# Banded attention's steps: projections ahead of scores, one product for the end, and a split moved from ScalarE to GpSimd

## The chip, the cores and the metric

The kernel runs on one core of a Trainium2 chip. The metric is the device time of one execution in microseconds (us); of several executions the median is told.

The engines have short names here: PE is TensorE, DVE VectorE, ACT ScalarE, POOL GpSimd and SP SyncE, which starts the DMAs. PEld is PE's loading of weights beside its matmuls.

## What is computed

The program holds two stacks of layers; the change touches one stage of the first, the odd layer with grouped-query attention in a window. Sizes: 1024 tokens, 256 context tokens, width 1024, 16 query heads on 4 key heads of dimension 64, query blocks of 128.

```python
def windowed_gqa(q, k, v, kc, vc, sink):
    ...
    s_ctx = jnp.einsum('bnqhgd,bchd->bnhgqc', qb, kc).astype(jnp.float32) * GQA_SCALE
    s_band = jnp.einsum('bnqhgd,bnkhd->bnhgqk', qb, kb).astype(jnp.float32) * GQA_SCALE
    ...
    valid = (jnp.abs(qpos - kpos) <= WINDOW) & (kpos >= 0) & (kpos < n)
    s_band = jnp.where(valid[None, :, None, None], s_band, -jnp.inf)
    s_sink = jnp.broadcast_to(sink[None, None, :, :, None, None], s_ctx.shape[:-1] + (1,))
    p = jax.nn.softmax(jnp.concatenate([s_ctx, s_band, s_sink], axis=-1), axis=-1).astype(v.dtype)
    ...
def odd_layer(h_lat, h_ctx, w_in, sink, w_out, rope, ctx_out):
    ...
    q, k, v, g = split_cols(h_lat @ w_in, ODD_SPLITS)
    q = apply_rope(q.reshape(b, n, GQA_KV_HEADS, GQA_GROUP, GQA_HEAD_DIM), *rope)
    ...
    y_l = (windowed_gqa(q, k, v, ck, cv, sink_hg) * jax.nn.silu(g)) @ w_out
```

## The kernel before

Numbers are float32, and each matrix product is made of three faster ones: a tensor x is split into a high half h (x rounded to a shorter type) and a low half l = x - h, and h*h, l*h and h*l are summed. So there are tiles in pairs: ah and al (features), whi and wlo (weights), kk and kl (keys), ph and pl (probabilities). `hi` (L162 on ACT, L164 on POOL) writes the high half and `lo` (L170) the low one.

The stage is `o1`, with `solo` set during attention. Keys, values and the first queries are projected ahead of it. Attention goes over 32 blocks (4 key heads by 8 query blocks); a block has 4 or 5 key tiles of 128 keys, and each key tile is one step of `attention`, 152 steps in all. A step puts together four kinds of PE work:

- D, scores: half-products of queries with keys (L1300 and L1301), eight for a block (four query heads of the group, with kk and with kl). They go into one of two PSUM buffers d. DVE adds the mask and takes the extreme (L1305); ACT takes the exponential (L1308, tile gw), and with that the buffer is free. `advance(want(n, i))` issues the halves, two or three in a step.
- F, projections: 28 products of queries or gates, each 24 matmuls of 512 columns (eight slices of the width by three halves; helper line L235), 4096 columns of fill for a product's accounts. `more` takes as many from the generator `fill` as a linear share of columns wants, three or six in a step (six where a step counts double). A product sums up in one PSUM bank f. A query is copied by ACT (L1113) and turned by POOL; a gate goes through tanh on ACT (L436) and a product on DVE (L437), and is written to DRAM (g_scr).
- V, values: two matmuls (L1328, L1329) with ph and pl into the bank o, of which there is one buffer.
- T, transposes: four (L1320) for the step two ahead, out of gw into the bank s; ACT makes ph (L162) and DVE pl (L170) from it.

After the exponentials of a step have been noted, `exps` issues them on ACT behind ph. When a block ends, `gqa_end` copies o into gatt (L1342, L1344) and adds up the sums of the exponentials in gden (L1348, L1349). Four blocks share one gden: it is transposed (L1354), turned into reciprocals (gdent), written to DRAM and read back spread over partitions, and POOL multiplies gatt by them (L1366).

`each`, called once in a step, is `add` in `o1`: it loads one gated feature (gate from g_scr, attention from am_scr), has POOL multiply the two (L1170), and in the next call `put` splits the product into ah and al for the output projection. The features of the first half of the tokens (c = 0) may start when `fill` puts them on the list `todo`, those of the second half (c = 1) when `fill` has come to its end. What is left after attention is done by a loop behind `self.solo = False`, then with products on DVE. The output projection's weights (`out_weights`: raw pieces by SP's DMAs, whi by ACT, wlo by POOL) follow, and its matmuls go into p.

PE, ACT and DVE carry out this stage in the order in which the code issues it (`in_order`); POOL's and SP's order is set by a scheduler.

Of the kernel before, what the change touches and what calls it, by code (L numbers as in the profile page):

```python
# [42 lines left out]
class Kern:  # L43
# [78 lines left out]
    def stg(self, n=512):  # L122
        return self.t(self.gp_, [P, 512], tag="stg", bufs=4)[:, 0:n]
# [175 lines left out]
    def attention(self, tiles, maxima, keys, prep, scores, values, end, want, fill, total, each, tail, late):  # L299


        steps = [(n, i) for n, t in enumerate(tiles) for i in range(len(t))]
        begin = [steps.index((n, 0)) for n in range(len(tiles))]
        G, U, done, cols, ahead, last, ends = {}, {}, 0, 0, [], None, iter(())

        def start(n):
            keys(n)
            G[n] = prep(n)

        def run(n):  # L310

            nonlocal done
            while n not in U:
                try:
                    next(G[n])
                    done += 1
                except StopIteration as e:
                    U[n] = e.value

        def advance(to):  # L320
            nonlocal done
            for n in range(len(tiles)):
                while done < min(to, sum(maxima[:n + 1])):
                    if n not in G:
                        start(n)
                    next(G[n])
                    done += 1

        def more(to):
            nonlocal cols  # L330
            while cols < to:
                n = next(fill, None)
                if n is None:
                    break
                cols += n
                if self.solo and cols % 4096 == 0 and to < total:
                    break
        for k in range(maxima[0] + maxima[1] - self.solo):
            if k == maxima[0] + min(self.R0, maxima[1]):
                run(0)  # L340
            advance(k + 1)
            more(cols + self.PRE * 512)
            self.exps()
        run(0)
        self.exps()
        first = cols

        share = [(2.0 if self.solo and i in (0, len(tiles[n]) - 2) else 1.0) for n, i in steps]
        whole = sum(share[:len(steps) - tail])
        for s in range(-2, len(steps)):  # L350
            swap = self.solo and s >= 0
            if self.solo and s >= 0:
                n, i = steps[s]
                advance(want(n, i))
                for m in range(n, len(tiles)):
                    if begin[m] - late <= s and m not in U:
                        run(m)
            if s + 2 < len(steps) and not swap:
                n, i = steps[s + 2]
                p, last = scores(U[n], tiles[n][i])  # L360
                ahead.append(p)
            if s < 0:
                continue
            n, i = steps[s]
            if not self.solo:
                advance(want(n, i))
            more(first + (total - first) * sum(share[:s + 1]) / whole)
            each()
            for m in range(n, len(tiles)):
                if begin[m] - late <= s and m not in U:  # L370
                    run(m)
            if i == 1 and not self.solo:
                with self.tc.issue_after(last):
                    next(ends, None)
            t = tiles[n]
            if i == 0:
                o = self.sps("o")
            values(o, U[n], t[i], i == 0, i == len(t) - 1, *ahead.pop(0))
            if i in (1, 2) and self.solo:
                next(ends, None)  # L380
            if i == len(t) - 1:
                ends = end(o, U[n])
                next(ends, None)
            if swap and s + 2 < len(steps):
                m, j = steps[s + 2]
                p, last = scores(U[m], tiles[m][j])
                ahead.append(p)
            self.exps()
        for _ in ends:
            pass  # L390
        more(total)
# [706 lines left out]
    def o1(self, act):  # L1098
# [9 lines left out]
        first = {}  # L1108
# [39 lines left out]
        mix = Act()  # L1148
# [3 lines left out]
        def add():  # L1152
            if made:
                k, c, gt = made.pop()
                self.put(mix, k, c, gt, "act", "pool" if k % 2 == 0 or self.solo else "dve")
                return
            kc = next((t for t in todo if t in self.ready), None)
            if kc is None:
                return
            todo.remove(kc)  # L1160
            k, c = kc
            ts = slice(*CH[c])
            gt = stg()
            self.dma(gt, g_scr[k * P:(k + 1) * P, ts])
            if k < 6:
                x = stg()
                self.dma(x, am_scr[k * P:(k + 1) * P, ts])
            else:
                x = self.last[c][:, k - 6]
            (nc.gpsimd if self.solo else V).tensor_tensor(gt, gt, x, ALU.mult)  # L1170
            made.append((k, c, gt))
# [42 lines left out]
        with self.in_order(), self.in_order(mybir.EngineType.Activation), self.in_order(mybir.EngineType.DVE):  # L1214
            self.gqa(gp, vv, k_scr, q_scr, am_scr, fill(), add)
# [5 lines left out]
        while todo or made:  # L1221
            add()
# [1024 lines left out]
```

## Time and profile before

| | us |
|---|---|
| median of 3 runs (2568.85 to 2571.87) | 2569.26 |
| profiled execution | 2569.92 |
| its span in the trace | 2568.1 |
| PE busy (share of the span) | 2391.3 (93%) |
| DVE busy | 1619.3 (63%) |
| ACT busy | 1112.8 (43%) |
| POOL busy | 938.6 (37%) |

The profile shows one execution. The busy times hold for the whole program, of which the attention stage lies from about 941 to 1398 us. A step of PE's work is followed on the time lines; what an engine waited for stands in square brackets behind the instruction that waited, with the time it was idle before it.

### The profile page before, as it was taken

The page shows a single profiled execution, that of the slowest core. Times are in us where ns is not written, and L with a number is a line of the kernel's source. Part 1 is how long each engine was busy: PE and PEld are TensorE (multiplying, and loading weights), DVE is VectorE, ACT ScalarE, POOL GpSimd, SP SyncE. Part 2 cuts the span into 40 slices and gives each one's busy share as a digit, 9 for nine tenths or more (in the row PEclk, how much of TensorE's full clock was granted, in tenths as well). Part 3 has the DMA queues.
Part 4 walks back from the last instruction along what each step waited for, and adds up shares of the span by engine and source line. Part 5 has one row for each costly group of instructions (what it writes and reads, how often), then busy time and mean ns, then how long its engine had stood idle before and what let it go on. Part 6 is the DMA issues. An engine that isn't in the chain of part 4 may idle for free. (4 is left out here: it accounts for less than half of the span.)

```text
span 2568.1 us, 36467 instructions
## 1 busy us (share of the span) xinstructions
PE 2391.3 (93%) x13014; PEld 1968.8 (77%) x13014; DVE 1619.3 (63%) x2732; ACT 1112.8 (43%) x2241; POOL 938.6 (37%) x776
## 2 busy tenths in 40 slices
PE   5999999999999998888887999999999999999998
PEld 3887777777678877776675879787777777799888
DVE  6785437788855546666665553558888577673455
ACT  4412226666653325555554323245666233513331
POOL 4304243354411145536333314046442343453231
PEclk9999999999999999999999999999999999999999
DMA  7465431132324221223214413233333232201433
GB/s 241 146 216 198 154 105 56 49 102 73 98 82 147 90 78 54 75 71 95 77 56 127 160 65 101 86 106 102 91 99 126 94 115 83 70 17 54 166 105 103
DMA packets 216693, 265.35 MB, mean 103 GB/s; under 512 B 42496, under 2 KB 142240, under 8 KB 216384
## 3 DMA queue, kind: packets, MB, share of 16 engines
q1 hardware_dynamic: 215792, 262.92, 32.5%
q8 instruction: 103, 1.69, 0.3%
q14 instruction: 78, 0.64, 0.1%
q10 hardware_dynamic: 720, 0.10, 0.0%
HBM read 188.83 MB, written 71.97 MB: 102 GB/s over the span
## 5 line engine op out<-in xcount | busy, mean ns | idle before, releaser
L170 POOL TENSOR_TENSOR wlo<-wraw,whi 128x512 fp32r<-128x512 f32 (+3 forms) x229 | 311.6, 1370 | 661.8 <-ACT whi L162 588.3
L162 ACT ACTIVATE whi<-wraw 128x512 fp32r<-128x512 f32 (+3 forms) x261 | 155.0, 613 | 346.7 <-DMA wraw<-in_even_w_in 50.8
L235 PE MATMUL f<-ah,whi 128*128 128x512 f32 x416 | 170.7, 410 | 7.5 <-DVE mixg L437 5.9
L170 DVE TENSOR_TENSOR pl<-pf,ph 128x512 fp32r<-128x512 f32 (+1 forms) x176 | 143.7, 817 | 41.3 <-ACT pf L1009 40.5
L235 PE MATMUL f<-ah,wlo 128*128 128x512 f32 x416 | 166.9, 401 | 0.0
L235 PE MATMUL f<-al,whi 128*128 128x512 f32 x416 | 166.4, 400 | 0.0
L162 ACT ACTIVATE ph<-s 128x512 fp32r<-128x512 f32 x152 | 90.8, 598 | 158.2 <-PE s L1320 157.2
L170 DVE TENSOR_TENSOR pl<-s,ph 128x512 fp32r<-128x512 f32 x152 | 104.4, 687 | 85.0 <-ACT ph L162 82.8
L1009 ACT ACTIVATE ph<-s 128x512 fp32r<-128x512 f32 (+1 forms) x176 | 101.5, 577 | 104.3 <-PE s L1006 103.3
L971 DVE TENSOR_REDUCE mx<-p 128x1 f32<-128x512 f32 (+1 forms) x208 | 116.8, 575 | 33.8 <-PE p L970 32.5
L235 PE MATMUL s<-ah,whi 128*128 128x512 f32 (+1 forms) x328 | 130.6, 398 | 3.9 <-ACT ah L545 3.2
L1305 DVE CUSTOM_DVE_ANT_0 d<-d,c_gqa_mask,nsink 128x640 f32<-128x640 f32 (+1 forms) x128 | 107.0, 853 | 39.1 <-PE d L1301 35.7
L235 PE MATMUL s<-al,whi 128*128 128x512 f32 (+1 forms) x328 | 128.8, 393 | 1.4 <-DVE al L547 1.4
L235 PE MATMUL s<-ah,wlo 128*128 128x512 f32 (+1 forms) x328 | 129.2, 394 | 0.0
L1696 DVE TENSOR_TENSOR_SCAN scu<-scu,ones_col 128x128 f32<-128x128 f32 (+3 forms) x64 | 97.6, 1538 | 14.1 <-ACT scu L1692 11.2
L1308 ACT ACTIVATE gw<-d,gm 128x640 f32<-128x640 f32 (+1 forms) x128 | 97.4, 765 | 14.1 <-DVE gm L1305 14.1
L1009 ACT ACTIVATE pf<-s 128x512 f32<-128x512 f32 (+1 forms) x176 | 100.9, 573 | 2.5 <-DVE pl L170 2.3
L1300 PE MATMUL d<-kk,qq 128*128 128x384 f32 (+1 forms) x128 | 48.5, 379 | 53.5 <-ACT gw L1308 46.1
L235 PEld LDWEIGHTS f<-ah,whi 128*128 128x128 f32 x416 | 79.3, 191 | 20.7 <-DVE mixg L437 8.5
L529 DVE CUSTOM_DVE_ANT_0 wmj<-wmt,srow,c_b_mod 128x1024 bf16<-128x1024 f32 x56 | 76.1, 1359 | 28.4 <-DMA wmt<-in_w_modT 26.1
L235 PEld LDWEIGHTS f<-ah,wlo 128*128 128x128 f32 x416 | 79.0, 190 | 17.7
L1320 PEld LDWEIGHTS s<-c_ident,gw 128*128 128x128 f32 x608 | 75.8, 141 | 21.1 <-DVE pl L170 0.5
(767 smaller groups left out, 7638.1 us busy)
## 6 DMA issues: line engine op xcount, KB each, us to landing
wmt<-in_w_modT SPq DMA_DIRECT2D x32, 512.0 KB
wraw<-in_even_w_in SPq DMA_DIRECT2D x56, 256.0 KB
wraw<-in_odd_w_in SPq DMA_DIRECT2D x48, 256.0 KB
wraw<-in_o_w_in SPq DMA_DIRECT2D x40, 256.0 KB
xold<-x_scr SPq DMA_DIRECT2D x40, 256.0 KB
mraw<-in_w_mod SPq DMA_DIRECT2D x16, 512.0 KB
x_scr<-x SPq DMA_DIRECT2D x32, 256.0 KB
mixx<-m_scr SPq DMA_DIRECT2D x30, 256.0 KB
```

What stands on the lines that cost most here:

```text
L162: nc.scalar.activation(out=out, in_=in_, func=AF.Copy)
L170: return e.tensor_tensor(out, in_, hi.bitcast(F32), ALU.subtract)
L235: self.nc.tensor.matmul(out, ws[:, k, c:c + m], a[k][ch], start=first and i == j == 0, stop=last and i == len(ks) - 1 and j == 2)
L529: V.tensor_tensor_reduce(out=junk, in0=w, in1=s[:, i], scale=0.5, scalar=self.bm[l][:, m, i:i + 1], op0=ALU.mult, op1=ALU.add, accum_out=s ...
L971: V.reduce_max(mx[:, e, j:j + 1], d[:, 0:y - x], axis=AX)
L1009: nc.scalar.activation(out=t, in_=s, func=AF.Exp, scale=MLA_SCALE)
L1300: mm(d[:, kw:kw + k1 - k0], qs, k[:, k0:k1], start=e == 0, stop=e == 1)
L1305: V.tensor_tensor_reduce(out=x, in0=x, in1=mask, scale=1.0, scalar=self.nsk[:, 4 * kv + g:4 * kv + g + 1], op0=ALU.add, op1=ALU.min, accum ...
L1308: self.pending.append(lambda w=w, x=x, g=g: nc.scalar.activation(out=w[:, 0:n], in_=x, func=AF.Exp, scale=-1.0, bias=m[:, g:g + 1], accum_ ...
L1320: self.nc.tensor.transpose(s[:, g * P:(g + 1) * P], W[g][:, x:x + P], self.ident)
L1696: V.tensor_tensor_scan(out=rev, data0=rev, data1=self.ones.to_broadcast([P, n]), initial=1.0, op0=ALU.mult, op1=ALU.mult)
```

## The change

In a step of the stage the projections (`more`) and the call of `each` now come ahead of the scores (`advance`); the loop that finishes a block's scores early, where they are due, stays behind them as before. In `attention` 4096 columns of `fill`, one product, are held back from the steps: the share that `more` asks for is capped, and behind the last step the end of the last block goes one part further (`next(ends)`), then `more(total + 1)` issues the kept product, and only then follows the transpose of the sums. As `fill` comes to its end only there, the features of the second half go on the list behind attention: all eight of them are made by the loop after it, where two were made inside before. Finally the high half of the features of the first half of the tokens is written by POOL in place of ACT: ACT has 8 instructions less, POOL 8 more; the two products that move out of the stage are on DVE now, not on POOL.

```diff
--- before.py
+++ after.py
@@ -347,14 +347,10 @@
 
         share = [(2.0 if self.solo and i in (0, len(tiles[n]) - 2) else 1.0) for n, i in steps]
         whole = sum(share[:len(steps) - tail])
+
+        held = 4096 if self.solo else 0
         for s in range(-2, len(steps)):
             swap = self.solo and s >= 0
-            if self.solo and s >= 0:
-                n, i = steps[s]
-                advance(want(n, i))
-                for m in range(n, len(tiles)):
-                    if begin[m] - late <= s and m not in U:
-                        run(m)
             if s + 2 < len(steps) and not swap:
                 n, i = steps[s + 2]
                 p, last = scores(U[n], tiles[n][i])
@@ -364,8 +360,10 @@
             n, i = steps[s]
             if not self.solo:
                 advance(want(n, i))
-            more(first + (total - first) * sum(share[:s + 1]) / whole)
+            more(first + (total - held - first) * min(1.0 if swap else 2.0, sum(share[:s + 1]) / whole))
             each()
+            if swap:
+                advance(want(n, i))
             for m in range(n, len(tiles)):
                 if begin[m] - late <= s and m not in U:
                     run(m)
@@ -386,6 +384,9 @@
                 p, last = scores(U[m], tiles[m][j])
                 ahead.append(p)
             self.exps()
+        if self.solo:
+            next(ends, None)
+            more(total + 1)
         for _ in ends:
             pass
         more(total)
@@ -1152,7 +1153,7 @@
         def add():
             if made:
                 k, c, gt = made.pop()
-                self.put(mix, k, c, gt, "act", "pool" if k % 2 == 0 or self.solo else "dve")
+                self.put(mix, k, c, gt, "pool" if self.solo else "act", "pool" if k % 2 == 0 or self.solo else "dve")
                 return
             kc = next((t for t in todo if t in self.ready), None)
             if kc is None:
```

PE, the step after one with three halves of scores. Before, the step's row begins behind four transposes (s): scores (d), six projections (f), values (o).

```order
L1320 MATMUL s_11754<-c_ident,gw_11616 128x128
L1300 MATMUL d_11765<-kk_10924,qq_11617 128x384
L1301 MATMUL d_11765<-kk_10924,qq_11617 128x256
L1300 MATMUL d_11765<-kl_10925,qq_11617 128x384
L1301 MATMUL d_11765<-kl_10925,qq_11617 128x256
L235 MATMUL f_11683<-ah_8655,whi_10606 128x512
L235 MATMUL f_11683<-al_8656,whi_10606 128x512
L235 MATMUL f_11683<-ah_8655,wlo_10607 128x512
L235 MATMUL f_11683<-ah_8661,whi_10606 128x512
L235 MATMUL f_11683<-al_8662,whi_10606 128x512
L235 MATMUL f_11683<-ah_8661,wlo_10607 128x512
L1328 MATMUL o_11716<-ph_11724,ovv_8682 128x512
```

After, in the like step (line numbers here are one higher than before), the projections stand directly behind the transposes.

```order
L1321 MATMUL s_11742<-c_ident,gw_11607 128x128
L235 MATMUL f_11715<-ah_8631,whi_10618 128x512
L235 MATMUL f_11715<-al_8632,whi_10618 128x512
L235 MATMUL f_11715<-ah_8631,wlo_10619 128x512
L235 MATMUL f_11715<-ah_8637,whi_10618 128x512
L235 MATMUL f_11715<-al_8638,whi_10618 128x512
L235 MATMUL f_11715<-ah_8637,wlo_10619 128x512
L1301 MATMUL d_11759<-kk_10918,qq_11608 128x384
L1302 MATMUL d_11759<-kk_10918,qq_11608 128x256
L1301 MATMUL d_11759<-kl_10919,qq_11608 128x384
L1302 MATMUL d_11759<-kl_10919,qq_11608 128x256
L1329 MATMUL o_11703<-ph_11711,ovv_8682 128x512
```

So six f rows have moved ahead of the d rows, and the values follow the scores.

PE, the end of the stage. Before, the values of the last two key tiles, then the transpose of the sums (gden) and the output projection (p):

```order
L1328 MATMUL o_13779<-ph_13787,ovv_8682 128x512
L1329 MATMUL o_13779<-pl_13788,ovv_8682 128x512
L1328 MATMUL o_13779<-ph_13805,ovv_8682 128x512
L1329 MATMUL o_13779<-pl_13806,ovv_8682 128x512
L1354 MATMUL s_13829<-c_ident,gden_13523 16x128
L235 MATMUL p_14005<-ah_13199,whi_13849 128x512
L235 MATMUL p_14005<-al_13200,whi_13849 128x512
```

After, the end of the kept product (its last 6 of 24 rows) stands ahead of the transpose of the sums:

```order
L235 MATMUL f_13786<-ah_8661,whi_12642 128x512
L235 MATMUL f_13786<-al_8662,whi_12642 128x512
L235 MATMUL f_13786<-ah_8661,wlo_12643 128x512
L235 MATMUL f_13786<-ah_8667,whi_12642 128x512
L235 MATMUL f_13786<-al_8668,whi_12642 128x512
L235 MATMUL f_13786<-ah_8667,wlo_12643 128x512
L1355 MATMUL s_13815<-c_ident,gden_13472 16x128
L235 MATMUL p_14005<-ah_13299,whi_13835 128x512
```

The transpose of the sums no longer follows the values but the 24 projections.

SP's queue, behind the reciprocals' DMAs (rec_scr) of the last key head's first half. wraw are raw pieces of the output weights, stg loads of features. Before:

```order
L129 DMA rec_scr<-gdent_13452 16x128
L129 DMA stg_13456<-rec_scr 64x4x128 x2
L129 DMA stg_13460<-rec_scr 64x4x128 x2
L129 DMA stg_13492<-g_scr 128x512
L129 DMA g_scr<-mixg_13488 128x512
L129 DMA stg_13494<-am_scr 128x512
L129 DMA stg_13551<-g_scr 128x512
L129 DMA wraw_13859<-in_o_w_out 128x2x256
L129 DMA stg_13603<-g_scr 128x512
L129 DMA wraw_13863<-in_o_w_out 128x2x256
```

After, from the second of the loads of reciprocals on:

```order
L129 DMA stg_13409<-rec_scr 64x4x128 x2
L129 DMA g_scr<-mixg_13430 128x512
L129 DMA stg_13461<-g_scr 128x512
L129 DMA stg_13463<-am_scr 128x512
L129 DMA stg_13520<-g_scr 128x512
L129 DMA stg_13522<-am_scr 128x512
L129 DMA stg_13577<-g_scr 128x512
L129 DMA stg_13579<-am_scr 128x512
L129 DMA stg_13638<-g_scr 128x512
L129 DMA stg_13684<-g_scr 128x512
L129 DMA wraw_13845<-in_o_w_out 128x2x256
L129 DMA wraw_13849<-in_o_w_out 128x2x256
```

The two pieces of weights, which stood between loads of features, now stand behind eight of them in a row.

ACT, at the same place. Before:

```order
L162 ACTIVATE ph_13504<-s_13499 128x512
L1308 ACTIVATE gw_13481,gs_13433<-d_13475,gm_13432 128x640
L162 ACTIVATE ah_13516<-stg_13492 128x512
L1342 ACTIVATE gatt_13522<-o_13388 64x2x128 x2
L162 ACTIVATE ph_13534<-s_13529 128x512
L162 ACTIVATE whi_13849<-wraw_13859 128x512
L162 ACTIVATE whi_13849<-wraw_13863 128x512
L162 ACTIVATE ph_13562<-s_13557 128x512
```

After:

```order
L437 ACTIVATE mixg_13604<-f_13457 128x512
L1343 ACTIVATE gatt_13471<-o_13504 64x2x128 x2
L162 ACTIVATE ph_13627<-s_13622 128x512
L162 ACTIVATE whi_13835<-wraw_13845 128x512
L162 ACTIVATE whi_13835<-wraw_13849 128x512
L162 ACTIVATE ph_13656<-s_13651 128x512
```

The feature's split (ah) is no longer between the exponential and the copy out of o (gatt); the splits of the weights (whi) stand as before between two splits of probabilities (ph).

## Rows read from the trace of the kernel before

**Rows 1.** Table by stretches: stretch, length, busy PE, PEld, DVE, ACT, POOL, clock, DMA.

```profile
941.00:1398.30 457.30, 388.18 (x2105) 319.72 (x2105) 281.26 (x573) 252.86 (x575) 196.75 (x188) 0.98 0.24 73
1363.60:1366.70 3.10, 3.08 (x9) 2.57 (x10) 3.07 (x6) 1.70 (x4) 2.17 (x2) 0.50 0.30 106
1397.40:1400.90 3.50, 3.00 (x7) 2.26 (x8) 1.99 (x4) 1.26 (x2) 0.00 (x0) 0.50 0.30 84
```

**Rows 2.** Waits from 935 to 1400 us: who waited for whom, total, times, longest.

```profile
PE d L1300 <- ACT gw L1308: 46.1, 30, 3.3
PE o L1328 <- DVE gatt L1344: 6.8, 5, 4.7
PE f L235 <- DVE mixg L437: 5.9, 11, 1.2
...
ACT ph L162 <- PE s L1320: 157.2, 109, 4.0
DVE pl L170 <- ACT ph L162: 82.8, 79, 3.3
```

**Rows 3.** Time lines of one step: start, length, engine, instruction, idle time before it.

```profile
1211.69 0.60 PE L1320 MATMUL s<-c_ident,gw 128*128 128x128 f32 x4
...
1212.82 0.79 ACT L1308 ACTIVATE gw<-d,gm 128x640 f32<-128x640 f32 x1
...
1213.75 0.44 PE L1300 MATMUL d<-kk,qq 128*128 128x384 f32 x1 [1.46 <-ACT gw L1308]
...
1214.44 0.39 PE L235 MATMUL f<-ah,whi 128*128 128x512 f32 x1
...
1215.83 0.40 PE L1328 MATMUL o<-ph,ovv 128*128 128x512 f32 x1
```

**Rows 4.** Time lines, the first of three borders between key heads.

```profile
1058.58 0.41 PE L1300 MATMUL d<-kk,qq 128*128 128x384 f32 x1 [1.16 <-POOL stg L450]
```

**Rows 5.** Groups of instructions: the gate's tanh and product (busy us, mean ns).

```profile
L436 ACT ACTIVATE mixg<-f 128x512 f32<-128x512 f32 x16 | 9.6, 597 | 7.7 <-PE f L235 7.6
L437 DVE SCALAR_TENSOR_TENSOR mixg<-mixg,f 128x512 f32<-128x512 f32 x16 | 11.0, 685 | 4.1 <-ACT mixg L436 4.0
```

**Rows 6.** Time lines: a feature's split on ACT, and values after it.

```profile
1361.11 0.63 ACT L162 ACTIVATE ah<-stg 128x512 fp32r<-128x512 f32 x1 [5.77 <-POOL stg L1170]
...
1363.62 0.77 PE L1328 MATMUL o<-ph,ovv 128*128 128x512 f32 x1 [4.71 <-DVE gatt L1344]
```

**Rows 7.** Time lines at the end of the stage.

```profile
1388.11 1.14 ACT L162 ACTIVATE whi<-wraw 128x512 fp32r<-128x512 f32 x2
...
1392.09 0.51 PE L1329 MATMUL o<-pl,ovv 128*128 128x512 f32 x1 [0.18 <-DVE pl L170]
...
1397.44 0.37 PE L1354 MATMUL s<-c_ident,gden 128*16 128x128 f32 x1 [4.85 <-DVE gden L1349]
...
1397.85 0.28 DVE L1356 TENSOR_SCALAR gdent<-s 16x128 f32<-16x128 f32 x1 [0.56 <-PE s L1354]
...
1398.27 0.77 PE L235 MATMUL p<-ah,whi 128*128 128x512 f32 x1 [0.46 <-ACT whi L162]
```

**Rows 8.** Time lines in the output projection: features' products, fourth weights, output 7.

```profile
1409.87 0.69 DVE L1170 TENSOR_TENSOR stg<-stg,stg 128x512 f32<-128x512 f32 x1
...
1421.54 1.15 DVE L1170 TENSOR_TENSOR stg<-stg,gatt 128x512 f32<-128x512 f32 x1 [0.84 <-DMA stg<-g_scr]
...
1434.02 2.67 POOL L170 TENSOR_TENSOR wlo<-wraw,whi 128x512 fp32r<-128x512 f32 x2 [7.51 <-ACT whi L162]
...
1435.95 0.39 PE L235 MATMUL p<-ah,whi 128*128 128x512 f32 x1
```

**Rows 9.** The small sums by line (ns min/median/max); scores behind the longest one.

```profile
L1349 DVE TENSOR_TENSOR gden<-gs,gm x30: 151/166/3036, 976.4 to 1381.3; 128x4 f32<-128x4 f32 x30
...
1159.99 0.39 PE L1300 MATMUL d<-kk,qq 128*128 128x256 f32 x1 [3.31 <-ACT gw L1308]
```

**Rows 10.** One line's answer: splits on POOL (ns min/median/max, first and last start).

```profile
L164 POOL TENSOR_SCALAR kk<-raw x9: 405/617/620, 973.8 to 1206.7; 128x512 fp32r<-128x512 f32 x6, 128x256 fp32r<-128x256 f32 x3
```

## The prediction

> **What bounds the kernel now.** Only the banded attention of the odd layer changes, so I read the stretch from its first step to the output projection. The table by stretches comes first: PE is busy 388.18 of 457.30 us at a granted clock of 0.98, ACT 252.86, DVE 281.26 [rows 1]. PE sets this stage and the other engines have room, so only PE's waits are to be won: 457.30 - 388.18 = 69 us, part of it small gaps. The list of waits names them. The largest by far is the first score matmul waiting for an exponential on ACT, 46.1 us in 30 waits; then value matmuls waiting for the o bank, 6.8 in 5, and projections waiting for the f bank, 5.9 in 11 [rows 2]. ACT for its part is idle 157.2 us for transposes and DVE 82.8 us for ACT [rows 2]: both wait for PE oftener than PE for them.
>
> The time lines show how one of the 30 waits comes about. Transposes start at 1211.69; the exponential that frees the score buffer runs from 1212.82 for 0.79 us; PE has finished its transposes and stands 1.46 us until the score matmul starts at 1213.75; the six projection matmuls behind it, which need nothing from ACT, start at 1214.44 and the values at 1215.83 [rows 3]. A block has two buffers for eight half-products, and the wait falls where a step with three halves is followed by the next step: once in a block.
>
> **Edit 1: projections ahead of scores.** What it moves: in each step F, D, V, T in place of D, F, V, T (projection, scores, values, transposes); on DVE the gate's product ahead of the score's reduction. Nothing is added. At the 30 places PE now does projections while the exponential ends. By the new order 24 of them have six projection matmuls ahead and 6 have three. Six take 1215.83 - 1214.44 = 1.39 us, three 0.70 [rows 3]. The wait is 1.46 [rows 3], so nearly all of it is covered: 24 x 1.39 + 6 x 0.70 = 37.6. At three borders between key heads a wait of 1.16 us of the same shape is put down to another releaser [rows 4]; each has three projections in the new order: 3 x 0.70 = 2.1. Together **-39.7 us**. The exponential itself stays where it is against the transposes: it follows them on ACT, and the reduction it waits for is DVE work on scores issued a step earlier. If it did come later by as much, nothing were won (second rival); above, the whole of the waits could go, 46.1 + 3.5 = 49.6.
>
> What the swap costs is at the borders of projection products. There is one f bank. The next product may start when ACT's tanh (0.597) and DVE's product (0.685) [rows 5] have read it; with hand-overs some 1.8 us after the last matmul has begun. Before, the scores and values stood in this gap; now a good part of that work stands ahead of the product's end, and the next product comes after two values (0.46) and transposes (0.60 [rows 3]), with D where there is one: 1.06 us and more. The 16 gate products at up to the longest wait seen, 1.2 [rows 2], give 19.2 at most against 5.9 now, that is +13.3; at best all 5.9 go. I take **+4**: most borders still have a part of V, T and D between them. The other bank, o, had 6.8 us of waits, of which 4.71 are one stall (edit 3) [rows 2, 6]; denser steps leave ACT and DVE less time to empty it: **+2**, with 0 and +6 as ends.
>
> **Edit 2: one product kept for the end.** 24 projection matmuls leave the loop, 24 x 0.232 = 5.6 us less there, and fill the stretch behind the last values. Before: last values at 1392.09, transpose of the sums after a wait of 4.85 at 1397.44, output projection at 1398.27 [rows 7], so 6.2 us. After: 0.2 + 23 x 0.232 = 5.6 to the last of the 24, 0.4 for its end, then what stands in a row: two splits of output weights on ACT, 1.14 [rows 7], which wait for the very weights that the kept product reads and stand ahead of its tanh, the tanh 0.60, the gate's product 0.69 [rows 5], the copy of the sums that DVE does behind it 0.28 and 0.2 of hand-overs: 8.9. The end gains 2.7 and the loop loses 5.6: -2.8. Besides, the clock: after the 4.85 us standstill the next 3.50 us ran at 0.50 [rows 1], that is 1.2 GHz; without standstill some 1.3 us of that come back. Together **-4.1**; between -6.6 (the splits find another place) and -1.5 (the clock falls all the same).
>
> **Edit 3: the high half of the first eight gated features on GpSimd.** Before, ACT stood 5.77 us ahead of such a split for GpSimd's product, and behind it in ACT's fixed order were the copies out of the o bank: PE's values waited 4.71 [rows 6], and 3.10 us then ran at 0.50 [rows 1], half of which is loss: 4.71 + 1.55 = 6.3 us that go. But the new wait stands near: GpSimd now has both halves, so the features come out more slowly, two more of them fall behind the reciprocals' DMAs, and on SP's queue the third and fourth piece of the first output weights now stand behind the features' loads. ACT's split of these pieces stands in its fixed order ahead of the next split of probabilities, so PE would wait again. No row shows it; it is bounded by 0 and by the stall that goes, 6.3; I take 2.5, nearer the lower end, since the pieces are asked for some microseconds ahead. Net **-3.8**.
>
> Later: the second eight features all fall behind the end in place of six. DVE's products there came at 1409.87 to 1421.54, five spacings, 2.33 us each [rows 8], so two more are 4.7. Behind them on GpSimd's list is the low half of the fourth output weights, which ran from 1434.02 for 2.67 us, to 1436.69, and its matmuls at output 7 started at 1435.95 without a wait, with no more than some 0.6 us of slack by what they read first [rows 8]. **+4.6**, between 0 (GpSimd takes the weights first) and 6.
>
> **Port of GpSimd and DVE.** The tiny sums on DVE take 0.166 us by median, but 3.04 us at the longest, where a GpSimd instruction runs beside it [rows 9]. PE's next score matmul then waited 3.31 in place of 1.46 [rows 9]: 1.85 paid. Eight more splits on GpSimd, 0.62 us each by the like split of keys [rows 10], add chances for this: **+1**, with 0 and 8 x 0.62 = 5 as ends. By the Trainium skill (SBUF — State Buffer, "SBUF: two separate sides") the port pair that GpSimd and DVE share is an exclusive lock: an instruction with two SBUF inputs on DVE stands until GpSimd's whole instruction is through, or the other way round. The trace agrees with its 3.04 us; by the rule's worst case the sum would be 4 us higher.
>
> **Sum.** -39.7 - 3.8 - 4.1 + 4 + 2 + 4.6 + 1 = -36.0. The profiled execution took 2569.92 (span 2568.1), the median of the three runs is 0.66 less: 2569.92 - 36.0 - 0.66 = **2533 us**.
>
> **Rivals.** *Nothing comes back:* the new waits at f, o and the fourth weights stay hidden, since ACT and DVE have idle time. The gain is 39.7 + 6.3 + 4.1 = 50.1 against the median: 2519. For it: ACT's 157.2 us of idle time [rows 2]; against: a single f bank, and half a microsecond of slack at the fourth weights. Chance 0.18.
>
> *The wait only moves:* the chain from exponential to reduction to the next exponential sets the step, and PE waits at F's end or at the values for what it waited for at the scores. Then only the end's 4.1 us remain: 2565, no difference that counts. Against it: DVE idles 82.8 us for ACT and ACT 157.2 for PE [rows 2], so neither is the bound of a block. Chance 0.07.
>
> *Slower, by the lock:* with the gate's product ahead of the reduction, DVE's sums at the block's end move against GpSimd's long products. If each of the 30 met one like the longest, PE would pay 30 x 1.85 = 55.5, less some 2.6 paid now: +53, so 2569.26 - 36 + 53 = 2586. From 36 / 30 = 1.2 us for a block on, the gain is gone. Against it: GpSimd is busy 196.75 of 457.30 us [rows 1], and the median sum is untouched. Chance 0.05.
>
> **How the numbers follow.** Forecast 0.70, the rivals 0.18, 0.07 and 0.05. The forecast's own ends: f between -5.9 and +13.3 and the other unknowns at their bounds, not all at once, 2522 to 2550. The range takes in the first rival with half of today's f waits gone, 2516, and on the other side 3 us more for an end of the f and o terms together: **2516 to 2553**. Within 0.2% is 5.1 us, about what can be told from no change. Faster 0.70 + 0.18 = 0.88, same 0.07, slower 0.05.
>
> **What would show it.** Score matmuls waiting for the exponential fall from 46.1 to about 10 us or less; the 4.71 stall at the values and ACT's 5.77 ahead of the feature split are gone; the stretch of 457.30 is near 417 to 420; 24 projections stand between the last values and the transpose of the sums, with the clock above 0.50 there; a wait of some 5 us appears at the fourth weights of output 7; projections' waits for the gate grow to about 10. I would be wrong if the exponentials start later against the transposes, if f waits pass 15 us, or if the tiny sums take over a microsecond on average.

## The result, and the profile after

The changed kernel took 2525.4 us, median of 6 runs (2520.4 to 2531.92), beside 2570.57 us for the kernel before: a ratio of 0.9824, with a 95% interval of 0.9808 to 0.984. That is 45 us or 1.8% faster. The forecast was 2533, with a range of 2516 to 2553.

The stage itself, from the first scores to the output projection (table by stretches: stretch, its length, busy time of PE, PEld, DVE, ACT and POOL, PE's clock, DMA):

```profile
944.65:1353.69 409.04, 384.45 (x2104) 315.35 (x2105) 281.58 (x572) 245.98 (x562) 196.25 (x191) 0.99 0.24 77
1354.60:1357.50 2.90, 2.90 (x8) 2.28 (x7) 0.00 (x0) 0.63 (x1) 0.95 (x1) 0.50 0.76 237
1397.71:1402.83 5.12, 5.12 (x14) 4.03 (x14) 3.98 (x6) 2.42 (x4) 2.56 (x2) 0.57 0.67 218
```

It takes 409.04 us in place of 457.30 [rows 1], with the same number of matmuls. The other two stretches are those with a lowered clock behind the start of the output projection and behind its wait at output 7. PE's waits from 935 to 1400 us (who waited for whom, total, times, longest):

```profile
PE f L235 <- DVE mixg L438: 8.5, 11, 3.4
PE p L235 <- ACT whi L162: 5.4, 1, 5.4
PE d L1301 <- issue: 5.2, 3, 3.7
PE d L1301 <- ACT gw L1309: 4.5, 6, 0.8
PE o L1329 <- DVE gatt L1345: 3.0, 5, 0.8
PE p L235 <- DVE gdent L1357: 2.4, 1, 2.4
...
PE o L1330 <- DVE pl L170: 2.0, 3, 1.6
```

Against [rows 2]: the scores' waits for the exponential are 4.5 us in 6 in place of 46.1 in 30, the o bank's 3.0 in place of 6.8, the f bank's 8.5 in place of 5.9. The 4.85 us at the transpose of the sums [rows 7] are gone. New are 2.4 us ahead of the output projection and 5.4 us at its output 7.

The place that answers to [rows 3], on the time lines (start, length, instruction):

```profile
1181.00 0.60 PE L1321 MATMUL s<-c_ident,gw 128*128 128x128 f32 x4
...
1181.35 0.48 PE L235 MATMUL f<-ah,whi 128*128 128x512 f32 x1
...
1182.13 0.79 ACT L1309 ACTIVATE gw<-d,gm 128x640 f32<-128x640 f32 x1
...
1183.06 0.44 PE L1301 MATMUL d<-kk,qq 128*128 128x384 f32 x1
...
1183.76 0.40 PE L1329 MATMUL o<-ph,ovv 128*128 128x512 f32 x1
```

The exponential starts 1.13 us after the transposes, as before (1212.82 - 1211.69), and the scores start 2.06 us after them, as before (1213.75 - 1211.69). In between six projections now run; the values follow the transposes by 2.76 us in place of 4.14.

The end of the stage, which answers to [rows 7]:

```profile
1345.10 0.50 PE L1330 MATMUL o<-pl,ovv 128*128 128x512 f32 x1 [0.17 <-DVE pl L170]
...
1351.04 0.27 PE L1355 MATMUL s<-c_ident,gden 128*16 128x128 f32 x1
1353.69 0.47 PE L235 MATMUL p<-ah,whi 128*128 128x512 f32 x1 [2.38 <-DVE gdent L1357]
```

From the last values to the output projection it is 8.59 us in place of 6.18. ACT and DVE in these 2.38 us do what was forecast, one behind the other:

```profile
1351.00 1.15 ACT L162 ACTIVATE whi<-wraw 128x512 fp32r<-128x512 f32 x2 [3.27 <-PE f L235]
1352.06 0.58 ACT L437 ACTIVATE mixg<-f 128x512 f32<-128x512 f32 x1
...
1352.67 0.69 DVE L438 SCALAR_TENSOR_TENSOR mixg<-mixg,f 128x512 f32<-128x512 f32 x1 [4.74 <-ACT mixg L437]
1353.28 0.27 DVE L1357 TENSOR_SCALAR gdent<-s 16x128 f32<-16x128 f32 x1
```

The fourth output weights and output 7, which answer to [rows 8]. The order of the lines is that of time; SPq is SP's DMA queue:

```profile
1386.16 0.95 DVE L1171 TENSOR_TENSOR stg<-stg,gatt 128x512 f32<-128x512 f32 x1 [1.03 <-DMA stg<-g_scr]
...
1387.15 0.63 ACT L162 ACTIVATE ah<-stg 128x512 fp32r<-128x512 f32 x1 [1.95 <-DVE stg L1171]
1387.69 1.14 ACT L162 ACTIVATE whi<-wraw 128x512 fp32r<-128x512 f32 x2
...
1390.96 0.38 SPq L129 DMA_DIRECT2D wraw<-in_o_w_out  x1
...
1397.03 0.63 ACT L162 ACTIVATE whi<-wraw 128x512 fp32r<-128x512 f32 x1 [2.69 <-DMA wraw<-in_o_w_out]
...
1397.71 0.79 PE L235 MATMUL p<-ah,whi 128*128 128x512 f32 x1 [5.39 <-ACT whi L162]
```

The last feature's product comes 32.5 us after the start of the output projection, against 23.3 before (1421.54 - 1398.27, [rows 7, 8]). Behind its split ACT splits the first two pieces of the fourth weights and GpSimd their low halves, which frees the raw buffers. SP, behind other loads in its order, starts the third piece at 1390.96; it lands, is split at 1397.03, and only then PE goes on: 5.39 us of wait, and 5.12 us at a mean clock of 0.57.

### The profile page after: what moved, and what is told of

Its sections match the earlier page's. It is cut to its first block, busy times and chain, and to the rows that moved or that the text cites. A ratio compares the mean times of both kernels' runs of the same rounds, so it can differ in the third digit from the quotient of the medians.

```text
span 2523.2 us, 36453 instructions
## 1 busy us (share of the span) xinstructions
PE 2388.5 (95%) x13014; PEld 1966.1 (78%) x13014; DVE 1621.3 (64%) x2734; ACT 1108.4 (44%) x2233; POOL 943.9 (37%) x782
## 5 line engine op out<-in xcount | busy, mean ns | idle before, releaser
L235 PE MATMUL f<-ah,whi 128*128 128x512 f32 x416 | 179.5, 432 | 10.3 <-DVE mixg L438 8.5
L170 DVE TENSOR_TENSOR pl<-pf,ph 128x512 fp32r<-128x512 f32 (+1 forms) x176 | 143.8, 818 | 41.4 <-ACT pf L1010 40.6
L235 PE MATMUL p<-ah,whi 128*128 128x512 f32 x224 | 91.5, 410 | 7.8 <-ACT whi L162 5.4
```

What stands on the lines that cost most here:

```text
L170: return e.tensor_tensor(out, in_, hi.bitcast(F32), ALU.subtract)
L235: self.nc.tensor.matmul(out, ws[:, k, c:c + m], a[k][ch], start=first and i == j == 0, stop=last and i == len(ks) - 1 and j == 2)
```

## The experiments

Two stretches of the trace tell the kernels apart better than the whole time does. **Stage** is from the first scores to the first matmul of the output projection, **first half** from there to the 193rd matmul recorded, the beginning of the second half of the tokens. Outside of these two, where the programs are alike, the profiled executions lie between 2047 and 2067 us, and up to 12 us apart on one chip. The two stretches vary too: between the two profiles of the changed kernel by 2.2 and 1.0 us, so a difference of some 2 us in the stage tells nothing. The times of the first four experiments stand beside runs of before with a median of 2570.42; the next four ran beside 2562.69, the last four beside 2565.76, so ratios are to be compared, not times.

| kernel | median, us | ratio to before (95%) | stage, us | first half, us |
|---|---|---|---|---|
| before | 2570.57 | 1 | 457.2 | 46.1 |
| changed | 2525.40 | 0.9824 (0.9808 to 0.9840) | 409.0 | 54.5 |
| edit 1 alone | 2524.97 | 0.9813 (0.9793 to 0.9833) | 415.5 | 46.8 |
| edit 2 alone | 2575.44 | 1.0018 (1.0003 to 1.0032) | 459.6 | 53.9 |
| edit 3 alone | 2566.93 | 0.9987 (0.9974 to 1.0000) | 449.4 | 47.3 |
| edits 1 and 2 | 2532.38 | 0.9852 (0.9835 to 0.9869) | 413.6 | 53.9 |
| edits 1 and 3 | 2514.24 | 0.9810 (0.9786 to 0.9833) | 410.1 | 46.7 |
| features 6, 7 first | 2511.55 | 0.9796 (0.9776 to 0.9816) | 409.1 | 44.9 |
| sums within the product | 2511.54 | 0.9806 (0.9785 to 0.9827) | 406.6 | 51.1 |
| both, weights ahead | 2510.52 | 0.9795 (0.9772 to 0.9818) | 405.1 | 45.0 |
| changed, again | 2524.87 | 0.9832 (0.9808 to 0.9856) | 406.9 | 53.5 |
| weights' split on POOL | 2521.97 | 0.9825 (0.9806 to 0.9844) | 407.6 | 54.5 |
| both, again | 2511.57 | 0.9777 (0.9756 to 0.9799) | 405.8 | 45.9 |
| both, and split on POOL | 2515.59 | 0.9801 (0.9779 to 0.9822) | 403.5 | 49.4 |

**Edit 1 alone.** The step's order of the change, put into the kernel before (the call of `each` moves with the projections and was not tried apart):

```diff
-            if self.solo and s >= 0:
-                n, i = steps[s]
-                advance(want(n, i))
...
             each()
+            if swap:
+                advance(want(n, i))
```

> Edit 1 alone: projections and the feature call ahead of the scores; no product kept, features split on ScalarE as before. Theory (the prediction's terms): scores' waits for the exponential fall by some 40 us or a little more, projections' waits for the gate grow by about 3, the 4.7 us stall at the values and the 4.8 us wait at the transpose of the sums stay, no wait at the fourth output weights: 2570 - 38 = about 2532. Rival (the wait only moves): values or projections wait as much in place of the scores, about 2566.

Measured: 2524.97 us, the whole of the change's gain and 7 us under the theory's time. The stage is 41.7 us shorter. PE's waits in it:

```profile
PE o L1324 <- DVE gatt L1340: 8.8, 6, 6.9
PE f L235 <- DVE mixg L433: 7.4, 12, 1.5
PE s L1350 <- DVE gden L1345: 4.9, 1, 4.9
...
PE d L1296 <- ACT gw L1304: 4.0, 5, 0.9
```

The scores' waits are gone, and neither the values nor the projections have taken them over: the rival of a wait that only moves falls. The stall at the values is there, 6.9 us now, and the 4.9 us at the transpose of the sums.

**Edit 2 alone.** The kernel before with `held`, the cap in `more` and the new lines behind the last step.

> Edit 2 alone: one product kept for the end, steps in the old order, split on ScalarE. Theory: the loop has 5.6 us less, the end 2.4 us more, but all eight features of the second half now stand behind the end and the fourth output weights come late by some 5 us of wait plus 2 to 3 us of slower clock behind it: 2570 - 3 + 8 = about 2575, slower than before. Rival (edit 2 pays for itself, the late weights come from the other edits): 2565 to 2567 and no wait at output 7.

Measured: 2575.44, slower by 0.18% (0.03 to 0.32%). The stage is not shorter (459.6), and the first half costs 8 us more, with the wait at output 7 there:

```profile
1438.46 1.14 ACT L162 ACTIVATE whi<-wraw 128x512 fp32r<-128x512 f32 x2
...
1449.37 0.63 ACT L162 ACTIVATE whi<-wraw 128x512 fp32r<-128x512 f32 x1 [3.32 <-DMA wraw<-in_o_w_out]
...
1450.05 0.50 PE L235 MATMUL p<-ah,whi 128*128 128x512 f32 x1 [3.56 <-ACT whi L162]
```

So edit 2 brings the late weights on its own. What the end gives the stage does not show beside variation of a few us. The stall behind the feature's split is still there, now with a score that waits 3.97 us in place of the values.

**Edit 3 alone.** `put` with POOL for the high half in `solo`, in the kernel before.

> Edit 3 alone: the high halves of the first features on GpSimd, all else as before. Theory: the 4.7 us stall of the values and the 3.1 us at half clock behind it go (6.3 us), one or two us come back as values waiting behind splits of output weights: about 2565. Rival (the stall is the feature's product, which is still late, and something else in ScalarE's order waits for it): 2570. Rival (GpSimd's extra work holds up small sums on VectorE): above 2572, with sums of over 1 us by line.

Measured: 2566.93, 3.5 us faster than before (the interval reaches just to no change). The stage is 7.8 us shorter, the values' longest wait for the o bank falls from 4.7 to 0.7, and a new one of 2.9 us at a score stands in the list:

```profile
PE d L1300 <- ACT gw L1308: 43.4, 30, 1.5
...
PE d L1300 <- POOL ah L164: 2.9, 1, 2.9
...
PE o L1328 <- DVE gatt L1344: 2.1, 4, 0.7
```

The list puts it down to the high half on POOL, but the time lines show ACT's order again: a split of output weights that waited 4.62 us for its piece, and behind it the exponential that the score needs.

```profile
1357.43 0.63 ACT L162 ACTIVATE whi<-wraw 128x512 fp32r<-128x512 f32 x1 [4.62 <-DMA wraw<-in_o_w_out]
...
1358.45 0.79 ACT L1308 ACTIVATE gw<-d,gm 128x640 f32<-128x640 f32 x1
...
1359.42 0.55 PE L1300 MATMUL d<-kk,qq 128*128 128x256 f32 x1 [2.89 <-POOL ah L164]
```

The reading of [rows 6] holds: the split in ACT's order made the stall, and with it gone the late weights make a smaller one. The clock behind it does not come back: from 1359.42 to 1362.30 it is at 0.50. Of the 7.8 us in the stage, 2.7 are scores' waits for the exponential (46.1 to 43.4): two long ones, at 980.65 and 1159.99 before, lie ahead of the first feature's product (1203) and so aren't this edit's work.

**Edits 1 and 2**, the changed kernel with the split on ACT again:

> The changed kernel without edit 3: split on ScalarE again. Theory: the stall at the values is back, since the copies out of the o bank stand behind the split in ScalarE's order; the time is that of the changed kernel plus 4 to 6: 2530. Rival (in the denser loop the product is there in time and the split costs nothing on ScalarE): 2525, no wait of over 2 us at the values.

Measured: 2532.38, 7 us above the changed kernel (5 by the ratio of its repetition; the intervals of the ratios overlap with either), and the stall is back, this time at the scores, since here an exponential stands behind the split:

```profile
1317.22 0.63 ACT L162 ACTIVATE ah<-stg 128x512 fp32r<-128x512 f32 x1 [6.74 <-POOL stg L1171]
...
1319.21 0.55 PE L1301 MATMUL d<-kk,qq 128*128 128x256 f32 x1 [4.30 <-POOL stg L1171]
```

So edit 3 is worth some 5 to 7 us on top of edits 1 and 2. The expectation named the values as the place; it is the scores. Beside edit 1 alone, on the same chip, these runs price edit 2 as well: 2532.38 against 2524.97, 7.4 us slower with it, and their intervals (0.9835 to 0.9869 and 0.9793 to 0.9833) do not meet.

**Edits 1 and 3**, the changed kernel without the kept product:

> The changed kernel without edit 2: no product kept for the end, so two features of the second half are made inside the stage again. Theory: the stage loses 3 us against the changed kernel (the loop has 24 projections more, the 4.8 us wait at the transpose of the sums is back), but from the output projection's start to its second half it takes 47 in place of 55 us: about 2520, 5 us faster than the changed kernel. Rival (the late fourth weights come from the denser loop and GpSimd's work): 55 us there again and about 2528.

Measured: ratio 0.9810, stage 410.1, first half 46.7. Without edit 2 the stage is 1.1 us longer and the first half 7.8 us shorter. On two stretches that is 6.7 us for leaving edit 2 out; in the ratios, 0.9810 against 0.9824 and 0.9832, the intervals overlap. Beside edit 1 alone (0.9813) the ratio shows nothing for edit 3, though the stage is 5.4 us shorter.

**Features 6 and 7 first.** One line, which changes no work, only the order in which the features of the second half are made:

```diff
-            todo.extend((k, 1) for k in range(8))
+            todo.extend((k, 1) for k in (6, 7, 0, 1, 2, 3, 4, 5))
```

> The changed kernel with the features of the second half made in the order 6, 7, 0 to 5 in place of 0 to 7. Features 6 and 7 read attention's last tile, and the space of the fourth output weights lies in what that tile leaves. Theory (the fourth weights wait for the last reader of that tile, not for the features as such): the wait of 5.4 us at output 7 and the slow clock behind it go, 47 us in place of 55 to the second half, about 2518. Rival (eight features in a row, their loads and splits, hold everything up): the wait stays above 3 us and the time is 2524 to 2526.

Measured: ratio 0.9796, first half 44.9 us, 9.6 us shorter than in the changed kernel. No wait at output 7. The pieces of the fourth weights are split far earlier against the start of the output projection (1350.86 here):

```profile
1374.77 0.64 ACT L162 ACTIVATE whi<-wraw 128x512 fp32r<-128x512 f32 x1
...
1383.95 0.64 ACT L162 ACTIVATE whi<-wraw 128x512 fp32r<-128x512 f32 x1 [1.55 <-DMA wraw<-in_o_w_out]
```

The last piece is there 33 us after that start, where the changed kernel had its third at 43. Eight features in a row still follow each other, so the rival falls: what held the weights was the last reader of attention's tile. That the reason is the space which this tile leaves is read from the program (the weights' pool is opened behind the closing of the attention's), and no run separates it from other ties between the two.

**Sums within the product.** The transpose of the sums after 12 of the 24 kept projections:

```diff
             next(ends, None)
+            more(total - 2048)
+            next(ends, None)
             more(total + 1)
```

> The changed kernel with the transpose of the sums after 12 of the 24 kept projections. Theory: the reciprocals and their DMAs start 4 to 5 us earlier, so the features do, and the wait at output 7 falls from 5.4 to 1 to 2 us; the output projection starts 0.5 to 1 us earlier, since the copy of the sums no longer stands behind the gate's product: about 2520. Rival (the features are paced by their loads and buffers, not by the reciprocals): the wait stays about 5 us, 2524.

Measured: ratio 0.9806, stage 406.6, first half 51.1. The 2.38 us ahead of the output projection are gone from the list of waits; the stage is 2.4 us shorter than in the changed kernel's first profile and 0.3 than in its second. The wait at output 7 is 3.5 us, neither the 1 to 2 of the theory nor the 5 of the rival: an earlier start of the features gives back a third. The interval of the ratio overlaps the changed kernel's.

**Both, and the fourth weights asked for ahead of the features:**

> Both of the last two: transpose of the sums within the kept product, features 6 and 7 first, and the fourth weights asked for ahead of the features. Theory: no wait at output 7, output projection up to 1 us earlier: about 2517, faster than the changed kernel by 8. Rival (the weights' loads ahead of the features' now make the second half of the output projection wait for features): 2520 or above, with waits of output projections for al or ah.

Measured: ratio 0.9795, as good as the order of the features alone (0.9796). In the repetition beside the changed kernel:

> The changed kernel once more, beside the others on one chip: ratio to the kernel before 0.982, the stretch from the first scores to the output projection about 409 us, from there to the second half of the output projection about 55 us, with 5 us of wait at output 7.

> The kernel with the transpose of the sums within the kept product, features 6 and 7 first and the fourth weights ahead of the features, beside the changed kernel: 405 us and 45 us in the two stretches, 10 to 14 us faster than the changed kernel on the same chip.

On that chip 2511.57 us (0.9777) against 2524.87 (0.9832) for the changed kernel: 13.3 us. Stage and first half together are 451.7 in place of 460.3 us, so 8.6 us are seen at the places aimed at. The other 5 are not seen in the traces: outside of the two stretches the profiled execution takes 6 us more than the changed kernel's. No kernel here is clearly faster than this one, and the order of the features alone can't be told from it.

**Weights' split on POOL.** The longest of the waits for the f bank has an engine's order behind it, on the time lines of the changed kernel:

```profile
1323.26 2.62 DVE L170 TENSOR_TENSOR wlo<-wraw,whi 128x512 fp32r<-128x512 f32 x2 [0.49 <-ACT whi L162]
...
1323.75 1.58 POOL L170 TENSOR_TENSOR al<-stg,ah 128x512 fp32r<-128x512 f32 x1
...
1326.53 0.50 PE L235 MATMUL f<-ah,whi 128*128 128x512 f32 x1 [3.35 <-DVE mixg L438]
```

VectorE splits two pieces of the first output weights ahead of the gate's product, beside a feature's split on GpSimd. Two such splits take VectorE 1.40 us where GpSimd is not at work (at 1365.65 in the same trace). The Trainium skill (SBUF — State Buffer, "SBUF: two separate sides") has one of the two engines stand while the other holds their common port; the stretching by 1.2 us, with the idle time inside the instruction's own duration, agrees with it. The edit gives that low half to POOL:

```diff
-            W[i] = self.wblk(w, i * 256, 256, pool=pool, leng="pool" if i % 2 else "dve")
+            W[i] = self.wblk(w, i * 256, 256, pool=pool, leng="pool" if i % 2 or (i == 0 and w is self.A["o_w_out"]) else "dve")
```

> The changed kernel with the low half of the first output weights on GpSimd in place of VectorE. There VectorE took 2.62 us for two of these splits ahead of the gate's product, and a projection waited 3.35 us. Theory (this split in VectorE's order, stretched beside GpSimd's feature work, holds the f bank and the values): the longest wait of a projection for the gate falls to 1.5 us or less and the slow clock behind it goes, 3 to 5 us faster than the changed kernel. Rival (GpSimd, already at work on eight features, now has the weights late): the output projection's first matmuls or its features come later and it is no faster or slower.

Measured: ratio 0.9825 against 0.9832, no difference. The longest wait for the gate did fall, from 3.1 us in the changed kernel's repetition to 1.8, but elsewhere:

```profile
PE f L235 <- DVE mixg L438: 6.6, 10, 1.8
...
PE o L1329 <- ACT ph L162: 1.8, 1, 1.8
```

The values now wait 1.8 us for a split of probabilities on ACT, which stands behind a split of the weights that waits 5.53 us for its piece. So the wait that was named went, and no time was won. The 5.53 us say that the pieces themselves are late; no run tests that. With the best kernel it is the same:

> The last one with the low half of the first output weights on GpSimd as well. Theory: a further 3 to 5 us, if the reading of the 3.35 us wait is right; rival: GpSimd is late, as fast or slower than without.

Measured: 0.9801 against 0.9777, intervals overlapping; the stage is 2.3 us shorter and the first half 3.6 us longer.

## Why the prediction was right, and where its steps were off

The time lay in the range and the sign was right; the forecast was 8 us too slow. By stretches the profiled executions give 409.0 - 457.2 = -48.2 us in the stage and 54.5 - 46.1 = +8.4 in the first half, -39.8 together (about -43 in the repetition); the sum had -40.6 and +4.6, -36. So the stage won 7.6 us more than forecast, the first half lost 3.8 us more, and the number profits from luck: two misses of opposite sign. Of the 7.6 us, 3.5 are in the waits that edit 1 takes and 3.5 in what the swap costs, both below. The rest of the 45 us lies where both programs are alike and varies from run to run. By the prediction's own steps:

- **Edit 1, -39.7: right.** The scores start 2.06 us after the transposes in both kernels, so what runs ahead of them is won in full: 1.39 us with six projections. Where there are three, 0.8 us of wait are left, and these six are the 4.5 us that remain. The scores' waits fell by 41.6 us and those at the three borders from 3.5 to 1.9, 43.2 together. The stage of edit 1 alone is 41.7 us shorter.
- **What the swap would cost was too high: +4, +2 and +1 were set.** The f bank's waits grew by 2.6 us in the changed kernel, by 1.5 in edit 1 alone. The o bank's, without the stall, grew from 2.1 to 3.0; in edit 1 alone they grew by 2.0 (8.8 against 6.8), all of it the one stall, which edit 3 takes. The small sums cost nothing more: the longest takes 1.42 us in the changed kernel against 3.04 [rows 9]; in edit 1 alone one takes 2.71 us, and still no score waits over 0.9 us there, so the projections ahead seem to cover such a delay too. What PE paid before, 1.85 us, went. The forecast put the 3.04 us down to one GpSimd instruction; the trace has three beside that sum, back to back from 1154.70 to 1157.78. In all some 3.5 us (2.6 at f, 0.9 at o) came of the 7 set.
- **Edit 3, -3.8: right in its parts.** The stall of 4.7 us went. What I put against it, 2.5 us for weights that stand behind the features' loads, is there: with edit 3 alone it is the 2.9 us at a score. In the changed kernel values waited 1.6 us for pl, in one of two profiles, and a projection 3.35 us for the gate behind the same weights' split; but that wait is over 3 us only in kernels with all three edits, and at most 2.0 us with edits 1 and 2 or 1 and 3 (2 and 3 were not run together), so it isn't edit 3's alone. The 1.55 us of clock did not come back in edit 3 alone. Alone it brought 3.5 us, on top of edits 1 and 2 some 5 to 7, and on top of edit 1 nothing that the ratios show.
- **Edit 2, -4.1: mis-sized.** The end took 8.59 us where 8.9 were forecast. The 1.3 us of clock were set as if PE no longer stood still there, though the forecast's own terms left 8.9 - 6.0 = 2.9 us of standing. After the 2.38 us that came, in place of 4.85, the stretch of 2.90 us still ran at 0.50; in the repetition of the same kernel the clock there stayed at 1.00. One thing in the edit's favour was overlooked: of the 4.85 us some 1.1 were the last sum, which took 1.23 us (1396.06 to 1397.29) beside a GpSimd split in place of 0.17, and with the kept product it takes 0.16. In all, the stage with edit 2 is between 3.3 us shorter and 2.3 us longer than without.
- **Fourth output weights, +4.6: the place was right, the mechanism half.** The wait came at output 7, from two features more behind the end, but I had put it on GpSimd's list, and it was ACT's order and SP's queue: the features' splits, the weights' first pieces, then the loads of the last. With the wait at 5.39 and the clock behind it the first half cost 8 us more, and 9 us of delay came from making the features, against 4.7 set: their spacing was 2.6 us, not 2.33 ((1386.16 - 1367.89) / 7 from the first product's start to the last one's), and the first came 2.6 us later. So edit 2 as a whole is a loss of some 5 to 7 us, where the sum of my two terms said 0.5: 4.6 alone by the ratio (0.8 to 8.2), 7.4 on top of edit 1, and 6.7 in the two stretches on top of edits 1 and 3. By this the change would have been better without it.

The rivals: nothing-comes-back, 2519, had the waits at f and o nearly right and missed the fourth weights; the other two didn't come. That GpSimd holds up VectorE is seen, at the splits of weights (2.62 us for two where a like one takes 0.69) and at the sums (10 of 32 took over 0.4 us, 8 before), but at the sums no score waited for it.

## What to carry to other kernels

Where an engine waits for another once in a block, look for work on it that waits for nobody and stands just behind: putting it ahead is worth its whole length, up to the length of the wait, if the awaited instruction's start doesn't depend on it. Before holding work back to fill a gap, list what is released by its end; here everything that waited for the kept product came later, and the gap came back as a wait 40 us behind. Among equal tasks do first the ones whose inputs hold space, or a buffer, that a later load needs.

## What the runs showed of the hardware

A standstill alone doesn't tell what the clock does behind it. The output projection started after the same wait of 2.38 us in both profiled executions of the changed kernel; the next 4 us ran at 0.58 in the one and at 1.00 in its repetition:

```profile
1353.69:1357.69 4.00, 4.00 (x11) 3.15 (x12) 0.83 (x1) 0.63 (x1) 1.67 (x2) 0.58 0.64 198
```

```profile
1345.39:1349.39 4.00, 4.00 (x17) 3.27 (x18) 0.83 (x1) 0.63 (x1) 1.66 (x2) 1.00 0.69 200
```

PE did 17 instructions in these 4 us in place of 11. With features 6 and 7 first, too, the wait was 2.38 us and the clock 1.00 behind it. So a microsecond or two of clock that is set against a removed wait is a guess: mine came true in one of two executions of the same kernel.

An instruction of VectorE that GpSimd holds up shows no idle time ahead of it; it only gets longer. The sum of 128x4 that takes 0.166 us by median took 3.04 us, from 1154.76 to 1157.80 in the kernel before, and ended 0.02 us behind the third of three GpSimd instructions that ran back to back.
